# Attention in a transformer block on one core: scores in three float32r passes over split queries and keys, reciprocals of the sums turned by a store and a load

## The chip, the core and the metric

The kernel runs on one core of a Trainium2 chip. A core has a matrix engine (TensorE, "PE" in the profile, with its weight loads as "PEld"), a vector engine (VectorE, "DVE"), a scalar engine (ScalarE, "ACT"), a general engine (GpSimd, "POOL") and a queue engine that issues transfers (SyncE, "SP"). Each works through its own instructions in program order, and they wait for one another by semaphores. Transfers run on 16 DMA engines. The metric is the device time of one execution in microseconds: 1033.1 before, the median of 3 runs (1032.53 to 1033.29).

## What is computed

One layer of a diffusion transformer, in float32: a modulated RMSNorm, an input projection, a token mixer (half pooling, half neighbourhood attention), an output projection, and a squared-ReLU MLP. The change lies in the attention of 1024 tokens on a 16 x 64 grid, with 8 heads of 64 and 256 context keys that every query sees:

```python
def row_block(r):
    ...
    s_loc = jnp.einsum('bnqhd,brnkhd->bhnqrk', q_r, k_b).astype(jnp.float32) * scale
    ...
    s_loc = jnp.where(col_mask, s_loc + bias.astype(jnp.float32), -jnp.inf)
    s_ctx = jnp.einsum('bnqhd,bkhd->bhnqk', q_r, k_ctx).astype(jnp.float32) * scale
    s = jnp.concatenate([s_loc.reshape(B, H, NA_NCB, NA_QB, n_loc), s_ctx], axis=-1)
    p = jax.nn.softmax(s, axis=-1).astype(v.dtype)
    p_loc = p[..., :n_loc].reshape(B, H, NA_NCB, NA_QB, kh, NA_KB)
    p_ctx = p[..., n_loc:]
    o = (jnp.einsum('bhnqrk,brnkhd->bnqhd', p_loc, v_b)
         + jnp.einsum('bhnqk,bkhd->bnqhd', p_ctx, v_ctx))
    return o.reshape(B, GRID_W, H, Dh)
```

## The kernel before

The large products run in float32r, a form of the operands in which a float32 value is split into a high part (a cast, `high_part` or `high`, on ScalarE) and a low part (value minus high, on VectorE). `three` (L197 to L200) multiplies high by high, high by low and low by high into one bank. The attention's own matmuls stay in float32.

*Ahead of the attention.* The projection of queries and keys is a seven-product scheme over quarter matrices; `kept_product` (L911 to L923) adds and subtracts the products into the pages `kT` (keys by head pair) and `q` (queries in blocks of 512 columns). The last products of the queries, P7 and P4, are computed by `last_query`: P7 just ahead of the loop, P4 within its first two turns. `tables(j)` (L867 to L883) makes the bias tables of head pair j: it loads U from `in_rpb` on SP's queue, and Pool subtracts it from a mask, 12 operations of 128 columns.

*The loop.* Pages of 128 x 1024 come from one pool of 33 (`page`), handed on when the last reader of the old content is done. A unit i is a head pair j = i / 8 and a column tile m = i % 8, 32 units in all; a tile's keys are those of itself and its neighbours (384 local columns for an inner tile, 256 at the edges) and 256 context columns. The loop runs N + 4 = 36 turns. Turn i holds, in this order:

- `tables` of the next pair, where m is 2; loads of output weights at turns 8, 16, 26 and 28 (`LOADS`); the six loads of the second half of the output weights at turn 32
- `weighed(i-4)` (L1070, VectorE): values times the reciprocals, into the heads' page
- modulation work: `mod_gate` at turn 4 (which stores `ga`), `column_sums` at turns 5 and 8 (storing and gathering `gsc`/`sc` and `gsh`/`s`), four accumulating transfers `y<-y` on Pool's queue in turns 1 and 2, the loads `ss<-y` on SP's at turns 5 and 6
- `low`, `mixed_split` (turns 8, 16, 24, 32) and `weight_split`: casts on ScalarE (L1082) and subtractions on VectorE (L1083)
- `scores(i)`: matmuls (L984, two heads on two halves of the rows), then on VectorE per head one custom operation, bias added and the extreme value found (L998)
- `turn(i-2)` (L1026): transposes of the exponentials, 64 x 64, and of the shares; `fifth_kept(i-2)` (L1040, ScalarE) copies what lies beside the banks
- `exps(i)` (L1007, ScalarE), with `turn_kept(i-2)` (L1045) in between: one copy of transposes on ScalarE, one on VectorE
- `share(i-1)`: the reciprocals of the sums (L1011) and their spread over 64 columns per head (L1013), both on VectorE
- `values(i-3)` (L1060, TensorE)

The program fixes the order within TensorE, ScalarE, VectorE and SP (`in_order`) and, over the loop, within Pool (`first_pool`). After the loop the mixed tokens go through the output projection (`out_sums`, `out_load`, accumulating `add_to` transfers on Pool's queue), whose first casts of the second half are `to_0h`, `to_1h`.

Of the kernel before, what the change touches and what calls it, by code (L numbers as in the profile page):

```python
# [80 lines left out]
def hybrid_block(ctx, tc, x, ctx_in, w_mod, b_mod, gp1, gp2, w_in, pool_w, rpb, w_out, w1, w2, vectors,  # L81
# [189 lines left out]
    with tc.tile_pool(name="ps1", bufs=6, space=PSUM) as ps1, tc.tile_pool(name="tmp1", bufs=3) as tmp:  # L271
# [614 lines left out]


        kT, qT = [None] * 4, [[None] * 2 for _ in range(4)]
        by_tile = lambda t: t.rearrange("p (m t) -> p m t", t=P)
        query = lambda j, b: by_tile(qT[j][b])[:, :, ::-1]  # L890

# [39 lines left out]
        with in_order(ET.PE, ET.Pool, ET.Activation, ET.DVE, ET.SP) as pooling:  # L931
            banks = {of: [bank(f"p{of}{j}") for j in range(2)] for of in "KQ"}
            use(-1)
            for step, (n, of, j) in enumerate([(n, of, j) for n, of in products for j in range(2)]):
                half_product(n, of, j, banks[of])
                use(step)
                if step in (5, 9, 17):
                    name = {5: "S1", 9: "S4", 17: "S3"}[step]
                    parts = token_operand(name, sraw[name])
                if step in (5, 7, 9, 11, 17, 19):  # L940
                    next(parts)
                    next(parts)
# [12 lines left out]

    with (
# [9 lines left out]
        sides = (pa[:, 256:448], pz[:, :192])  # L966


        def scores(i):
            j, m = units[i]  # L970
            inner = 0 < m < NM - 1
            n = NKEY if inner else 4 * P
            o = 1 if m == 0 else 0
            q = qT[j][m // 4]
            cols = slice((m % 4) * P, (m % 4 + 1) * P)
            heads = [slice(e * HD, (e + 1) * HD) for e in range(2)]
            S = [ps_s.tile([P, 1024], F32, tag="S", name=f"S{j}_{m}_{e}") for e in range(2)]
            if inner:
                parts = ((128, kT[j][:, (m - 1) * P : (m + 2) * P]), (512, kc[:, j, :]))
            else:  # L980
                parts = ((0, kc[:, j, :]), (256, kT[j][:, (m + o - 1) * P : (m + o + 1) * P]))
            for c0, keys in parts:
                for e, hs in enumerate(heads):
                    nc.tensor.matmul(S[e][:, c0 : c0 + keys.shape[1]], q[hs, cols], keys[hs], start=True, stop=True)  # L984
            halves = lambda a: a.rearrange("p (a b) -> p a b", a=2)
            for e in range(2):
                t = tabs[j % 2][e]
                sp = att.tile([P, NKEY], F32, tag="sp", name=f"sp{j}_{m}_{e}", bufs=6)[:, :n]
                if inner:
                    s, bt, to = S[e][:, 128:768], t[:, :NKEY], sp  # L990
                else:
                    s, to = halves(S[e][:, 0:512]), halves(sp)
                    if o:
                        bt = halves(t[:, 2 * P : 8 * P])[:, :, P:]
                    else:
                        bt = halves(t[:, NLOC : NLOC + 512])
                nm = sm(f"nm_{i}_{e}", 1, 6)
                nc.vector.tensor_tensor_reduce(out=to, in0=s, in1=bt, scale=1.0, scalar=BIG, op0=add, op1=ALU.min,  # L998
                                               accum_out=nm)
                probs[i, e] = sp  # L1000
                least[i, e] = nm
# [7 lines left out]
        def share(i):  # L1009
            ri = sm(f"ri_{i}", 2, 2)  # L1010
            nc.vector.reciprocal(ri, sums[i])  # L1011
            shares[i] = att.tile([P, P], F32, tag="ri", name=f"rb{i}", bufs=2)
            nc.vector.tensor_copy(shares[i].rearrange("p (e t) -> p e t", e=2),  # L1013
                                  ri.rearrange("p (e o) -> p e o", o=1).to_broadcast([P, 2, HD]))

        def turn(i):
            inner = 0 < units[i][1] < NM - 1
            t = [bank(f"T{i}_{h}") for h in range(2)]  # L1020
            turned[i] = t
            halves = [slice(h * HD, (h + 1) * HD) for h in range(2)]

            def both(to, src):
                for h, hs in enumerate(halves):
                    nc.tensor.transpose(to(h), src(hs), ident[hs, hs])  # L1026

            both(lambda h: sides[h][:, :HD], lambda hs: shares[i][hs])
            for e in range(2 if inner else 0):
                both(lambda h: sides[h][:, (e + 1) * HD : (e + 2) * HD], lambda hs: probs[i, e][hs, 4 * P : 5 * P])  # L1030
            for c in range(4):
                for e in range(2):
                    o = (4 * e + c) * HD
                    both(lambda h: t[h][:, o : o + HD], lambda hs: probs[i, e][hs, c * P : (c + 1) * P])

        def fifth_kept(i):
            n = (3 if 0 < units[i][1] < NM - 1 else 1) * HD
            fifths[i] = att.tile([P, 384], F32, tag="px", name=f"px{i}", bufs=4).rearrange("p (h t) -> p h t", h=2)
            for h in range(2):
                nc.scalar.copy(fifths[i][:, h, :n], sides[h][:, :n])  # L1040

        def turn_kept(i, h, copy):
            if h == 0:
# [4 lines left out]
        def values(i):  # L1048
            j, m = units[i]
            vc = [vcp[:, 0:512], vcp[:, 512:1024]]  # L1050
            if 0 < m < NM - 1:
                vs = vb[m - 1 : m + 2] + vc
            else:
                o = 1 if m == 0 else 0
                vs = vc + vb[m + o - 1 : m + o + 1]
            cols = slice((i % 2) * P, (i % 2 + 1) * P)
            for c, v in enumerate(vs):
                for e in range(2):
                    f = (2 * j + e) * HD
                    nc.tensor.matmul(pa[e * HD : (e + 1) * HD, cols], v[:, f : f + HD],  # L1060
                                     turns[i][:, e, c] if c < 4 else fifths[i][:, :, (e + 1) * HD : (e + 2) * HD],
                                     start=(c == 0), stop=(c == len(vs) - 1))


        def weighed(i):
            j, m = units[i]
            if m == 0:
                heads[j] = page(f"f{j}")
            to = heads[j].rearrange("p (m h t) -> p m h t", h=2, t=HD)[:, m, ::-1, ::-1]
            nc.vector.tensor_tensor(to, pa[:, (i % 2) * P : (i % 2 + 1) * P].rearrange("p (h t) -> p h t", h=2),  # L1070
                                    fifths[i][:, :, :HD], mul)

        N = len(units)

# [77 lines left out]
        with in_order(ET.PE, ET.Activation, ET.DVE, ET.SP) as projected:  # L1152

            def last_query(n, j):
                half_product(n, "Q", j, last_queries)
                kept_product(n, "Q", j, last_queries[j])

            for j in range(2):
                last_query("P7", j)
            for i in range(N + 4):  # L1160
                if i < N and units[i][1] == 2 and units[i][0] < 3:
                    tables(units[i][0] + 1)
                if i in LOADS:
# [827 lines left out]
```

## Time and profile before

| | |
|---|---|
| median of 3 runs | 1033.1 us (1032.53 to 1033.29) |
| the profiled execution: span | 1030.8 us |
| TensorE busy | 1017.8 us, 99% of the span |
| VectorE busy | 751.8 us, 73% |
| ScalarE busy | 543.7 us, 53% |
| Pool busy | 110.7 us, 11% |
| attention loop, first scores of unit 0 to those of unit 31 | 218.90 to 319.35 us |

A span is what lies between the first and the last instruction of the profiled execution; the runs' times are taken around it. Rows of a timeline read: start in us, length in us, engine, line of the kernel, operation, output <- inputs, partitions x elements, number of instructions in the group, and in brackets the idle time before it with what ended it. Matmuls overlap with the next one, so the distance between two starts, not the length, is what one costs. In the chain of waits each piece has its start, its length and the work. Rows of transfers give queue, number, size of each and median time from issue to landing.

### The profile page before, as it was taken

How to read it: one execution, taken by the hardware profiler on the slowest of the kernel's cores; microseconds unless marked ns; L12 is line 12 of the kernel's file. 1: busy time of each engine (PE TensorE's matmuls, PEld its weight loads, DVE VectorE, ACT ScalarE, POOL GpSimd, SP SyncE). 2: the span in 40 equal slices, each digit the busy share in tenths (PEclk: the TensorE clock that was granted, in tenths of full speed). 3: DMA queues.
4: the chain of work that ended last, by engine and by line, in shares of the span. 5: the costliest groups of instructions: out<-in, count | busy, mean ns of one | idle time of the engine just before them, and what ended most of it. 6: DMA issues, size and time to landing. Idle time of an engine off the chain costs nothing.

```text
span 1030.8 us, 15588 instructions
## 1 busy us (share of the span) xinstructions
PE 1017.8 (99%) x5782; PEld 834.2 (81%) x5782; DVE 751.8 (73%) x1187; ACT 543.7 (53%) x941; POOL 110.7 (11%) x168
## 2 busy tenths in 40 slices
PE   8999999999999999999999999999999999999997
PEld 6788888877887888888888888888888888888885
DVE  5588767858996587878998887855766666547576
ACT  7573255328887556776655544555543334334431
POOL 3011200244311311310000000000000000000001
PEclk9999999999999999999999999999999999999999
DMA  9999798632337866795786666637967766555556
GB/s 343 332 255 338 246 265 296 204 86 80 72 95 194 203 180 200 253 237 168 267 269 210 204 210 214 205 122 241 327 220 271 248 226 220 202 180 189 176 182 211
DMA packets 123132, 222.68 MB, mean 216 GB/s; under 512 B 9456, under 2 KB 55152, under 8 KB 123056
## 3 DMA queue, kind: packets, MB, share of 16 engines
q1 hardware_dynamic: 96560, 171.14, 50.4%
q0 software_dynamic: 9360, 19.58, 9.5%
q10 hardware_dynamic: 17136, 30.97, 8.0%
q8 instruction: 45, 0.74, 0.3%
q14 instruction: 31, 0.25, 0.1%
HBM read 168.16 MB, written 52.45 MB: 214 GB/s over the span
## 4 chain that ended last, share of the span: by engine, by line
PE 95%; DMA 2%; ACT 1%; DVE 1%; issue 0%; SPq 0%; DVEq 0%; POOLq 0%; ACTq 0%
PE pu L449 4%; PE S L984 4%; PE pa L1060 3%; PE phv L198 3%; PE phz L198 3%; PE phx L198 3%; PE pyx L198 3%; PE phx L200 3%; PE phv L199 3%; PE phx L199 3%; PE pyx L199 3%; PE pyx L200 3%; PE pyv L199 3%; PE pyv L198 3%; PE pyz L199 3%; PE pyz L198 3%
## 5 line engine op out<-in xcount | busy, mean ns | idle before, releaser
L1007 ACT ACTIVATE sp<-sp,nm 128x640 f32<-128x640 f32 (+1 forms) x64 | 51.4, 803 | 20.0 <-DVE nm L998 19.6
L1577 ACT ACTIVATE c<-c 128x512 f32<-128x512 f32 x48 | 30.3, 632 | 47.0 <-DVE c L1697 28.2
L146 ACT CAST wpS<-S 128x512 fp32r<-128x512 f32 x64 | 38.7, 616 | 26.4 <-PE phv L200 9.2
L198 PE MATMUL phx<-thB,wpA 128*128 128x512 f32 x128 | 50.2, 392 | 0.0
L200 PE MATMUL phx<-thB,wpA 128*128 128x512 f32 x128 | 49.8, 389 | 0.0
L199 PE MATMUL phx<-tlB,wpA 128*128 128x512 f32 x128 | 49.8, 389 | 0.0
L152 DVE TENSOR_TENSOR wpS<-S,wpS 128x512 fp32r<-128x512 f32 x64 | 43.4, 685 | 8.3 <-ACT wpS L146 8.3
L998 DVE CUSTOM_DVE_ANT_0 sp<-S,tab 128x640 f32<-128x640 f32 (+1 forms) x56 | 42.9, 803 | 8.8 <-PE S L984 7.3
L1578 ACT ACTIVATE c<-c 128x512 f32<-128x512 f32 x48 | 30.3, 631 | 15.1 <-DVE sa L1660 12.3
L140 POOL TENSOR_TENSOR ry<-vy,nhalf 128x1 f32<-128x1 f32 x8 | 5.9, 740 | 280.7 <-DVE vy L138 280.7
L198 PEld LDWEIGHTS phx<-thB,wpA 128*128 128x128 f32 x128 | 24.0, 188 | 5.5 <-ACT s L1628 0.5
L984 PE MATMUL S<-kT,q 64*128 64x384 f32 (+1 forms) x128 | 27.9, 495 | 0.3 <-DVE nm L998 0.3
L200 PEld LDWEIGHTS phx<-thB,wpA 128*128 128x128 f32 x128 | 24.0, 188 | 5.0
L199 PEld LDWEIGHTS phx<-tlB,wpA 128*128 128x128 f32 x128 | 24.0, 188 | 4.9
L1060 PE MATMUL pa<-pt,v 128*64 128x128 f32 x352 | 25.9, 279 | 0.6 <-ACT px L1040 0.2
L1045 DVE COPY pt<-T 128x512 f32<-128x512 f32 x32 | 22.0, 686 | 5.5 <-PE T L1026 5.5
L198 PE MATMUL phv<-thT,wpA 128*128 128x512 f32 x64 | 25.1, 392 | 0.0
L198 PE MATMUL phz<-thB,wpS 128*128 128x512 f32 x64 | 25.0, 391 | 0.0
L200 PE MATMUL phv<-thT,wpA 128*128 128x512 f32 x64 | 24.9, 389 | 0.0
L199 PE MATMUL phv<-tlT,wpA 128*128 128x512 f32 x64 | 24.9, 389 | 0.0
L200 PE MATMUL phz<-thB,wpS 128*128 128x512 f32 x64 | 24.9, 389 | 0.0
L199 PE MATMUL phz<-tlB,wpS 128*128 128x512 f32 x64 | 24.9, 389 | 0.0
(1100 smaller groups left out, 3359.7 us busy)
## 6 DMA issues: line engine op xcount, KB each, us to landing
b<-in_w SPq DMA_DIRECT2D x64, 512.0 KB, 4.2
hrS<-hdS SPq DMA_DIRECT2D x32, 512.0 KB, 5.1
hrA<-hdA SPq DMA_DIRECT2D x24, 512.0 KB, 5.5
wm<-in_w_mod SPq DMA_DIRECT2D x16, 512.0 KB, 9.7
wa_0w<-in_w SPq DMA_DIRECT2D x16, 512.0 KB, 5.3
wa_1w<-in_w SPq DMA_DIRECT2D x16, 512.0 KB, 4.5
hdA<-c ACTq DMA_DIRECT2D x32, 256.0 KB, 2.8
hdS<-sa ACTq DMA_DIRECT2D x32, 256.0 KB, 2.7
```

Of the source, the lines that this page charges most:

```text
L146: nc.scalar.copy(hi, src)
L152: nc.vector.tensor_tensor(lo, src, hi.bitcast(F32), sub)
L198: nc.tensor.matmul(ps, ahi, bhi, start=first, stop=False, skip_group_check=more)
L199: nc.tensor.matmul(ps, ahi, blo, start=False, stop=False, skip_group_check=more)
L200: nc.tensor.matmul(ps, alo, bhi, start=False, stop=last, skip_group_check=more)
L449: nc.tensor.matmul(pus[b][j], wk(wgt, k, low, j * P, P), r, start=(k == 0 and n == 0), stop=(k == KT - 1 and n == 2))
L984: nc.tensor.matmul(S[e][:, c0 : c0 + keys.shape[1]], q[hs, cols], keys[hs], start=True, stop=True)
L998: nc.vector.tensor_tensor_reduce(out=to, in0=s, in1=bt, scale=1.0, scalar=BIG, op0=add, op1=ALU.min, accum_out=nm)
L1007: nc.scalar.activation(sp, sp, AF.Exp, bias=least[i, e], scale=-1.0, accum_out=sums[i][:, e : e + 1])
L1060: nc.tensor.matmul(pa[e * HD : (e + 1) * HD, cols], v[:, f : f + HD], turns[i][:, e, c] if c < 4 else fifths[i][:, :, (e + 1) * HD : (e + ...
L1577: nc.scalar.activation(r, src, AF.Relu)
L1578: nc.scalar.activation(r, r, AF.Square)
```

## The change

Queries and keys are split into high and low parts: `parts_of` casts 512 columns on ScalarE and subtracts on VectorE, or on Pool where the engine is given. There are 16 such splits, and the context keys' page is split once, 128 x 1024. One split of keys and one of queries are made in the projection stage, four right ahead of the loop, two in turn 2 on VectorE, and eight in turns 3 to 6, whose subtractions go to Pool. `scores` runs three passes over each part. Since a key page now has 512 columns, tiles 3 and 4, whose keys lie in two pages, have three parts in place of two.

The reciprocals are no longer spread by a VectorE copy and transposed by TensorE: `share` stores the 128 x 2 reciprocals to memory on SP's queue, transposed, and `spread`, one turn later, loads each head's row into 64 partitions, two transfers on SP's queue. `weighed` multiplies by what was loaded. `turn` loses its transposes of the shares, and `fifth_kept` copies 128 columns in place of 192 for inner units and nothing for edge units.

```diff
+        keys, queries, kcs = {}, {}, []
+
+        def parts_of(to, j, b, small=False, engine=None):
+            name = f"{'k' if to is keys else 'q'}P{j}_{b}"
+            src = kT[j][:, b * 512 : (b + 1) * 512] if to is keys else qT[j][b]
+            t = whl.tile([P, 1024], F32R, tag="hl", name=name) if small else page(name, F32R)
+            hi, lo = to[j, b] = t[:, :512], t[:, 512:]
+            nc.scalar.copy(hi, src)
+            (engine or nc.vector).tensor_tensor(lo, src, hi.bitcast(F32), sub)
...
+                if step == 10:
+                    kcs += [page(f"kc{n}", F32R) for n in "hl"]
+                    split(kcp, *kcs)
+                if step == 20:
+                    parts_of(keys, 0, 0)
+                if step == 22:
+                    parts_of(queries, 0, 0, True)
...
-            if inner:
-                parts = ((128, kT[j][:, (m - 1) * P : (m + 2) * P]), (512, kc[:, j, :]))
-            else:
-                parts = ((0, kc[:, j, :]), (256, kT[j][:, (m + o - 1) * P : (m + o + 1) * P]))
-            for c0, keys in parts:
-                for e, hs in enumerate(heads):
-                    nc.tensor.matmul(S[e][:, c0 : c0 + keys.shape[1]], q[hs, cols], keys[hs], start=True, stop=True)
+            t0, t1 = (m - 1, m + 2) if inner else (m + o - 1, m + o + 1)
+            at = 128 if inner else 256
+            local = []
+            for b in range(2):
+                b0, b1 = max(t0, 4 * b), min(t1, 4 * b + 4)
+                if b0 < b1:
+                    local.append((at + (b0 - t0) * P, [a[:, (b0 - 4 * b) * P : (b1 - 4 * b) * P] for a in keys[j, b]]))
+            parts = local + [(512, ck)] if inner else [(0, ck)] + local
+            for c0, k in parts:
+                for n_q, n_k in ((0, 0), (0, 1), (1, 0)):
+                    for e, hs in enumerate(heads):
+                        nc.tensor.matmul(S[e][:, c0 : c0 + k[0].shape[1]], q[n_q][hs, cols], k[n_k][hs],
+                                         start=(n_q + n_k == 0), stop=(n_q == 1))
...
-            shares[i] = att.tile([P, P], F32, tag="ri", name=f"rb{i}", bufs=2)
-            nc.vector.tensor_copy(shares[i].rearrange("p (e t) -> p e t", e=2),
-                                  ri.rearrange("p (e o) -> p e o", o=1).to_broadcast([P, 2, HD]))
+            inverse[i] = dram.tile([2, P], F32, tag=f"inv{i % 6}", name=f"inv{i}")
+            nc.sync.dma_start(inverse[i].rearrange("e t -> t e"), ri)
+
+        def spread(i):
+            shares[i] = att.tile([P, P], F32, tag="ri", name=f"rb{i}", bufs=4)
+            for e in range(2):
+                nc.sync.dma_start(shares[i][e * HD : (e + 1) * HD], inverse[i][e : e + 1, :].to_broadcast([HD, P]))
...
-            both(lambda h: sides[h][:, :HD], lambda hs: shares[i][hs])
...
-            n = (3 if 0 < units[i][1] < NM - 1 else 1) * HD
-            fifths[i] = att.tile([P, 384], F32, tag="px", name=f"px{i}", bufs=4).rearrange("p (h t) -> p h t", h=2)
+            if not 0 < units[i][1] < NM - 1:
+                return
+            fifths[i] = att.tile([P, 256], F32, tag="px", name=f"px{i}", bufs=4).rearrange("p (h t) -> p h t", h=2)
             for h in range(2):
-                nc.scalar.copy(fifths[i][:, h, :n], sides[h][:, :n])
+                nc.scalar.copy(fifths[i][:, h], sides[h])
...
             nc.vector.tensor_tensor(to, pa[:, (i % 2) * P : (i % 2 + 1) * P].rearrange("p (h t) -> p h t", h=2),
-                                    fifths[i][:, :, :HD], mul)
+                                    shares[i].rearrange("p (h t) -> p h t", h=2), mul)
...
+            parts_of(keys, 0, 1, True)
+            parts_of(queries, 1, 0, True)
+            parts_of(keys, 1, 0, True)
+            parts_of(keys, 1, 1)
+            later = [(to, 2, b, True) for b in range(2) for to in (keys, queries)]
+            later += [(to, 3, b, False) for b in range(2) for to in (keys, queries)]
             for i in range(N + 4):
+                if i == 2:
+                    for j in range(2):
+                        parts_of(queries, j, 1)
+                if 3 <= i < 7:
+                    for _ in range(2):
+                        parts_of(*later.pop(0), nc.gpsimd)
...
+                if 1 < i <= N + 1:
+                    spread(i - 2)
                 if 0 < i <= N:
                     share(i - 1)
```

More of the change, by code (lines that the diff above doesn't have):

```diff
@@ L965, in hybrid_block @@
         pa, pz = (ps_o.tile([P, 512], F32, tag=n, name=n) for n in ("pa", "pz"))
-        sides = (pa[:, 256:448], pz[:, :192])
+        sides = (pa[:, 256:384], pz[:, :128])
+        inverse = {}
         def scores(i):
@@ L973, in scores @@
             o = 1 if m == 0 else 0
-            q = qT[j][m // 4]
+            q = queries[j, m // 4]
+            ck = [a[:, j * CTX : (j + 1) * CTX] for a in kcs]
             cols = slice((m % 4) * P, (m % 4 + 1) * P)
@@ L1026, in both @@
                     nc.tensor.transpose(to(h), src(hs), ident[hs, hs])
-            both(lambda h: sides[h][:, :HD], lambda hs: shares[i][hs])
             for e in range(2 if inner else 0):
-                both(lambda h: sides[h][:, (e + 1) * HD : (e + 2) * HD], lambda hs: probs[i, e][hs, 4 * P : 5 * P])
+                both(lambda h: sides[h][:, e * HD : (e + 1) * HD], lambda hs: probs[i, e][hs, 4 * P : 5 * P])
             for c in range(4):
@@ L1060, in values @@
                     nc.tensor.matmul(pa[e * HD : (e + 1) * HD, cols], v[:, f : f + HD],
-                                     turns[i][:, e, c] if c < 4 else fifths[i][:, :, (e + 1) * HD : (e + 2) * HD],
+                                     turns[i][:, e, c] if c < 4 else fifths[i][:, :, e * HD : (e + 1) * HD],
                                      start=(c == 0), stop=(c == len(vs) - 1))
```

## The prediction

> **What bounds the kernel now.** I read the page's head and its chain of waits first, then the chain through the attention stage, a table of busy time by stage, and last one unit of the loop instruction by instruction. A unit is one column tile of one pair of heads; there are 32, and the loop starts one per turn.
>
> ```profile
> span 1030.8 us, 15588 instructions
> ...
> PE 95%; DMA 2%; ACT 1%; DVE 1%; issue 0%; SPq 0%; DVEq 0%; POOLq 0%; ACTq 0%
> ```
>
> 95% of the chain is TensorE work, so time taken off TensorE comes off the end, as long as the others can follow. In the chain through the stage (start, length, what), these are the scores of units 8 and 31:
>
> ```profile
> 247.44 1.06 PE S L984 x8
> ...
> 319.35 1.06 PE S L984 x8
> ```
>
> 23 units in 71.91 us: 3.127 us each. The stage's table (PE, PEld, DVE, ACT, Pool busy) tells what stands behind TensorE:
>
> ```profile
> 240.00:260.00 20.00, 20.00 (x306) 16.03 (x304) 17.34 (x54) 17.42 (x48) 10.30 (x22) 1.00 0.14 28
> ```
>
> VectorE and ScalarE are each busy 87% of it: there is little room before they would bind. One unit on TensorE and then on VectorE:
>
> ```profile
> 262.84 0.92 PE L984 MATMUL S<-kT,q 64*128 64x384 f32 x4
> ...
> 263.59 0.60 PE L984 MATMUL S<-kcT,q 64*128 64x256 f32 x4
> ...
> 264.02 0.22 PE L1026 MATMUL pa<-ident,rb 64*128 64x64 f32 x1
> ...
> 266.04 0.92 PE L984 MATMUL S<-kT,q 64*128 64x384 f32 x4
> ```
> ```profile
> 264.22 0.82 DVE L998 CUSTOM_DVE_ANT_0 sp<-S,tab 128x640 f32<-128x640 f32 x1
> ...
> 266.32 0.16 DVE L1011 RECIPROCAL ri<-su 128x2 f32<-128x2 f32 x1
> ...
> 266.65 0.28 DVE L1070 TENSOR_TENSOR f<-pa,px 128x128 f32<-128x128 f32 x1
> ```
>
> From start to start: 0.75 us for the local scores, 0.43 for those on the context, 2.02 for transposes and values; 3.20 in all. VectorE's part of a unit runs from 264.22 to 266.93 (266.65 + 0.28), 2.71 us.
>
> **The change, part by part.** *Scores.* Each f32 matmul stands in the trace as two instructions (x4 for two heads), whose heads run side by side; the change makes three float32r passes of it. The nearest float32r rows:
>
> ```profile
> 85.16 0.28 PE L690 MATMUL pkc<-hc,wk0l 128*128 128x256 f32 x1
> 85.28 0.39 PE L690 MATMUL pkc<-hc,wk0h 128*128 128x512 f32 x1
> 85.50 0.28 PE L690 MATMUL pkc<-hc,wk0l 128*128 128x256 f32 x1
> ```
>
> Above, two f32 passes of 256 columns take 0.43, or 0.84 ns a column and pass; 384 would take 0.64, and the other 0.11 of the 0.75 is the first pass's start. In float32r 256 columns take 0.12 and 512 take 0.22, 0.43 to 0.47 ns a column. An inner unit becomes 3 x (0.165 to 0.18) + 3 x (0.11 to 0.12) + 0.11 = 0.93 to 1.01, against 1.18: -0.2. By the same rates the 8 edge units (256 + 256 columns) win 0.14; 8 others cross the new 512-column pages and have three short parts, which is worth between nothing and 0.17, taken as 0.09. The mean over 16, 8 and 8 units is -0.16. The transposed pair of shares goes too, one of 33 steps between 264.02 and the values: -0.06 as the trace spaces these first pairs. TensorE's own period becomes 2.91; 2.8 to 3.05 are its ends, since no row has float32r on 64 rows with two heads side by side.
>
> *The other engines.* VectorE loses the copy of the shares (0.14 to 0.23), ScalarE two narrow slices, so VectorE comes to about 2.5 a unit and ScalarE, whose 87% of 3.127 is 2.72, to a little less than that. They can follow 2.91, but not much below 2.75.
>
> *The splits, and what waits for Pool.* The 16 splits of 512 columns cost a cast and a subtraction each. These rows have the same shapes, and show where the loop stood (ScalarE, then VectorE):
>
> ```profile
> 247.89 0.62 ACT L1082 CAST mix<-f 128x512 fp32r<-128x512 f32 x1
> ```
> ```profile
> 227.77 0.15 DVE L1011 RECIPROCAL ri<-su 128x2 f32<-128x2 f32 x1
> ...
> 249.87 0.69 DVE L1045 COPY pt<-T 128x512 f32<-128x512 f32 x1
> ...
> 251.00 0.68 DVE L1083 TENSOR_TENSOR mix<-f,mix 128x512 fp32r<-128x512 f32 x1
> ```
>
> Those in the projection stage run under TensorE's products: nothing (without that cover 3 x 0.65). Four subtractions ahead of the loop, 4 x 0.68 = 2.7, stand on VectorE before the first unit's bias; TensorE still has a projection product of 3 us between units 0 and 1, so some 0.6 to 0.9 reaches the first reciprocal (227.77 becomes 228.4), and the two of the third turn add 1.4. The eight of turns 3 to 6 go to Pool, two a turn, with two casts (1.24) a turn on ScalarE. What Pool and SP's queue do there now:
>
> ```profile
> 221.28 4.95 POOL L883 TENSOR_TENSOR tab<-msk,U 128x128 f32<-128x128 f32 x12 [10.47 <-DMA U<-in_rpb]
> 226.17 1.69 POOL L188 DMA_DIRECT2D y<-y  x2
> 234.52 1.99 POOL L253 DMA_DIRECT2D ga<-acca  x4 [6.67 <-DVE acca L247]
> 238.68 1.91 POOL L253 DMA_DIRECT2D gsc<-accsc  x4 [2.17 <-ACT accsc L621]
> 242.22 0.93 POOL L623 DMA_DIRECT2D sc<-gsc  x1 [1.63 <-DMA gsc<-accsc]
> ```
> ```profile
> 216.89 1.19 SPq L876 DMA_DIRECT2D U<-in_rpb  x2
> ```
>
> SP runs in program order, and the store of unit 0's reciprocals comes ahead of the load of U for the second pair's bias table. So that load, issued at 216.89 now, waits for the first reciprocal and the store's issue: about 228.4 + 0.15 + 0.42 = 229.0. Pool's table started 4.39 after the issue (221.28), so it starts at 233.4, ends at 238.4, and the two y accumulations end at 240.1; only then come the subtractions. One of 512 columns on Pool has no row: the table's 128-column ones come every 4.95/12 = 0.41, so four times that, 1.65, is the upper bound; the lower is VectorE's 0.68 for that shape, since nothing here shows Pool ahead of VectorE. I take 1.35, near the upper end, whose rows are Pool's own, less 0.3 for what is paid once instead of four times. In Pool's order four subtractions precede the ga stores, two the gsc stores, and two follow the sc gather: the sixth ends at 240.1 + 6 x 1.35 + 2.0 = 250.2, the seventh at 240.1 + 7 x 1.35 + 1.99 + 1.91 + 1.63 + 0.93 = 256.0, the eighth at 257.4.
>
> Who waits: a page is handed on when its last reader is done, and by the program's order the mix cast of the eighth turn (247.89) needs the seventh subtraction's page, and the copy of unit 6's transposes (249.87) the eighth's. They would come 8.1 and 7.5 late. Behind them on ScalarE and VectorE stand the next unit's exponentials and biases, and TensorE waits for those. A second path is nearly as late: the ss load of turn 6 waits on SP for the ga stores (issued by 240.1 + 4 x 1.35 + 2.0 = 247.5), and the shares of unit 4 stand behind it. I take 7.5 us of delay at unit 8, with 3 (subtractions of 0.68: the seventh at 251.3) and 10 (1.65: 8 x 0.3 more) as ends.
>
> The Trainium skill, "GPSIMD Engine Reference", section 3.1 (Elementwise — side-by-side cycle accounting), has a two-input operation on Pool at about 2.6 cycles an element, 4497 ns for 2048 elements. By that I estimate 1.2 us for 512; the eighth would end at 256.2 and the sum would be 1.2 lower. By the same estimate 128 elements need about 0.28, and the trace's 0.41 is above it, so I stay with the row.
>
> *The reciprocals' way over memory.* Each unit's 128 x 2 values are stored as 256 separate elements; two loads spread them over 64 partitions each a turn later. On SP the loads of unit k wait for its store to have landed, and the next store is queued behind them. So a turn of SP is store to landing + two issues. Nearest rows: a small store and a gather (size, time to landing), and the issues of a small broadcast load (least, median and most ns):
>
> ```profile
> gsc<-accsc POOLq DMA_DIRECT2D x4, 1.0 KB, 1.6
> ...
> sc<-gsc POOLq DMA_DIRECT2D x1, 4.0 KB, 3.0
> ```
> ```profile
> L243 SPq DMA_DIRECT2D gpa<-in_gp x4: 347/416/698, 201.9 to 203.5; - x4
> ```
>
> 1.6 in whole rows, 3.0 for 1024 single elements: for 256 elements I take 2.0, plus 2 x 0.42, plus some 0.1: 2.9 a unit (2.4 to 3.9). There is time in a unit's own account: a reciprocal is due 3.5 after its scores (266.32 - 262.84), the weighting 0.56 after those of three turns later, so 3 x 2.9 - 3.1 = 5.6 for store, issues and loads, 2.0 + 0.8 + 2.0 with loads like stores.
>
> *The end of the loop.* Six loads of 512 KB for the output weights stand between the last reciprocals' transfers on SP. Before, the first was issued and, after an accumulation by Pool, used by ScalarE at
>
> ```profile
> 308.06 0.37 SPq L1143 DMA_DIRECT2D to_0w<-in_w_out  x1
> ```
> ```profile
> 340.57 1.05 ACT L146 CAST to_0h<-to_0w 128x1024 fp32r<-128x1024 f32 x1
> ```
>
> Behind unit 30's store (its reciprocal is due 3.5 after 319.35, so 323 and the delay) the cover of 32.5 us shrinks to some 17, which still has to hold a load and an accumulation. I put 1.0 on it (0 if both fit, 4 if they need 21).
>
> *The sum.* From unit 8 on the period is the greater of TensorE's 2.91 and SP's 2.9, which take turns: I take 2.95, 0.177 less than now, times 24 = 4.2 back. 1030.8 + 7.5 - 4.2 + 1.0 = 1035.1 of span. The runs' median, 1033.1, is 2.3 above the profiled span; with that, 1037.4.
>
> **The rivals.** *SP sets the period.* If a store takes 2.6 or more to land, SP's turn is 2.6 + 0.84 + 0.1 = 3.5, over what TensorE needs today. Then nothing comes back and 24 x 0.35 = 8 is added: 1033.1 + 7.5 + 8 = 1048.6. For it: the 3.0 of single elements, and the loads of 512 KB among which these small ones run. Against it: there are a quarter as many elements. It decides from a landing of 2.2 (period 3.13). The Trainium skill, "DMA: Bandwidth & Descriptors", speaks for this rival: under Specifications it has transfers below 512 bytes as read-modify-write, and under Rules for kernel authors many small transfers are to be made one large one. No row here shows a 4-byte store.
>
> *Faster: the delay is hidden and TensorE keeps its gain.* If Pool's subtraction is below 0.9, the eighth ends by 253.8, 3.9 late, as long as the path by the ss load is no later; and with passes of 0.16 and 0.11 and a landing below 1.8 (whole rows have 1.6), the period falls to 2.8, TensorE's lower end. Then 24 x 0.327 = 7.8 comes back: 1033.1 + 4.5 - 7.8 = 1029.8. For it: TensorE is the chain at 95%. Against it: 0.41 for 128 columns would have to be mostly fixed cost.
>
> *The scores don't get shorter.* Three passes are fewer than two f32 ones only if float32r on half the rows, with short columns, keeps 0.47 ns a column. If it went at the rate of f32, the 1.07 of the passes would grow by half, 0.54, less 0.06 for the shares: period 3.6, 1033.1 + 7.5 + 24 x 0.48 = 1052. Against it: the rows at 256 columns keep the rate.
>
> **How the numbers follow.** The forecast's own range: delay 5.5 to 9.9, period 2.9 to 3.1: 1033 to 1044. Chances: forecast 0.48, SP's period 0.25, faster 0.20, scores no shorter 0.04; 0.03 for what I don't see. The range, 1029.5 to 1050, takes in the lower end of all costs (1033.1 + 3 - 6.6 at a period of 2.85) and SP's rival. A difference counts from 0.2%, about what a measurement of this kernel can tell: 1031.0 and 1035.2. Below that: 0.15 from the faster case and 0.02 of the forecast; between: 0.05 of the faster case and 0.13 of the forecast; the rest is slower, 0.65.
>
> **What would show it.** The second pair's U load issued near 229 and its table starting near 233; the mix cast of the eighth turn idle behind Pool and near 255; unit 8's scores at 255, not 247.4. Pool's subtraction of 512 columns at 1.35. From unit 8 on 2.95 from scores to scores, scores at 0.95 to 1.0. SP's stores landing in 2.0; over 2.2, and weighting idle behind rb, would show the first rival. I am wrong in the main step if unit 8 is less than 3 late, or if the period stays at 3.1 for a reason other than SP.

## The result, and the profile after

The changed kernel takes 1246.24 us (median of 4 runs, 1245.58 to 1249.75) against 1033.12: a ratio of 1.2071, interval 1.2056 to 1.2086. It is 213 us slower, where 4 were forecast. The page of the profile after, its span, its chain by engine and by line:

```profile
span 1247.9 us, 15982 instructions
...
PE 72%; DMA 23%; SPq 3%; DVE 1%; issue 1%; ACT 0%; DVEq 0%; POOLq 0%; ACTq 0%
DMA inv<-ri 20%; PE pu L449 4%; DMA rb<-inv 3%; SPq L1042 2%; PE phv L198 2%; PE phz L198 2%; PE phx L198 2%; PE pyx L198 2%; PE pyv L200 2%; PE phv L199 2%; PE phz L199 2%; PE phx L199 2%; PE pyz L200 2%; PE pyx L200 2%; PE phx L200 2%; PE
```

A fifth of the chain is one kind of transfer, the store of the reciprocals (`inv<-ri`). All of the loss lies in the attention loop: the last unit's weighting, on VectorE, first before and then after:

```profile
337.35 0.28 DVE L1070 TENSOR_TENSOR f<-pa,px 128x128 f32<-128x128 f32 x1
```
```profile
555.12 0.29 DVE L1098 TENSOR_TENSOR f<-pa,rb 128x128 f32<-128x128 f32 x1 [2.89 <-DMA rb<-inv]
```

It comes 217.8 us later, and the spans differ by 217.1. What SP waited for in the loop (line, releaser, us in total, times, longest), and two turns of SP's queue:

```profile
SPq L1042 <- DMA inv<-ri: 227.5, 30, 9.5
```
```profile
406.63 1.09 SPq L1042 DMA_DIRECT2D rb<-inv  x2
407.77 0.59 SPq L1037 DMA_DIRECT2D inv<-ri  x1
416.20 1.09 SPq L1042 DMA_DIRECT2D rb<-inv  x2
417.39 0.53 SPq L1037 DMA_DIRECT2D inv<-ri  x1
```

A store is issued at 407.77, the loads behind it at 416.20, 8.43 later, when it has landed; two issues of 1.09 together, and the next store goes at 417.39. A turn is 9.6 us, and one unit is done per turn. TensorE is busy for half of such a stretch (PE, PEld, DVE, ACT, Pool busy, the granted clock, share of the DMA engines):

```profile
400.00:440.00 40.00, 20.21 (x208) 17.51 (x208) 11.25 (x30) 11.19 (x30) 5.87 (x12) 0.63 0.26 28
```

Its granted clock is 0.63 here, 1.00 in the same loop before; but TensorE is not what SP's turn waits for. Transfers of the stage, first before and then after (number, size, median from issue to landing):

```profile
wor<-in_w_out SPq DMA_DIRECT2D x4, 512.0 KB, 3.7
...
U<-in_rpb SPq DMA_DIRECT2D x6, 244.5 KB, 3.9
...
ga<-acca POOLq DMA_DIRECT2D x4, 1.0 KB, 2.4
```
```profile
rb<-inv SPq DMA_DIRECT2D x64, 32.0 KB, 3.5
wor<-in_w_out SPq DMA_DIRECT2D x4, 512.0 KB, 10.7
...
U<-in_rpb SPq DMA_DIRECT2D x6, 244.5 KB, 11.3
...
inv<-ri SPq DMA_DIRECT2D x32, 1.0 KB, 8.4
...
ga<-acca POOLq DMA_DIRECT2D x4, 1.0 KB, 10.2
```

The 1 KB store lands in 8.4 us, and `wor`, `U` and `ga`, which have nothing to do with it, land 7 to 8 us later than before, the last of them on Pool's queue. Not every transfer does: `gsh` lands in 1.8 (the median), against 2.2 before.

### The profile page after: what moved, and what is told of

The parts are those of the page before. It is cut to its first block, busy times and chain, and to the rows that moved or that the text cites. A ratio compares the mean times of both kernels' runs of the same rounds, so it can differ in the third digit from the quotient of the medians.

```text
span 1247.9 us, 15982 instructions
## 1 busy us (share of the span) xinstructions
PE 1073.1 (86%) x5894; PEld 887.8 (71%) x5894; DVE 754.0 (60%) x1164; ACT 548.1 (44%) x942; POOL 120.1 (10%) x176
## 4 chain that ended last, share of the span: by engine, by line
PE 72%; DMA 23%; SPq 3%; DVE 1%; issue 1%; ACT 0%; DVEq 0%; POOLq 0%; ACTq 0%
DMA inv<-ri 20%; PE pu L449 4%; DMA rb<-inv 3%; SPq L1042 2%; PE phv L198 2%; PE phz L198 2%; PE phx L198 2%; PE pyx L198 2%; PE pyv L200 2%; PE phv L199 2%; PE phz L199 2%; PE phx L199 2%; PE pyz L200 2%; PE pyx L200 2%; PE phx L200 2%; PE pyv L198 2%
## 5 line engine op out<-in xcount | busy, mean ns | idle before, releaser
L1054 PE MATMUL pa<-ident,sp 64*128 64x64 f32 x48 | 11.4, 334 | 116.3 <-DVE f L1098 116.3
L1098 DVE TENSOR_TENSOR f<-pa,rb 128x128 f32<-128x128 f32 x32 | 9.3, 292 | 147.1 <-DMA rb<-inv 145.5
L1054 PEld LDWEIGHTS pa<-ident,sp 64*128 64x128 f32 x48 | 6.9, 196 | 122.1 <-DVE f L1098 122.1
L1088 PE MATMUL pa<-pt,v 128*64 128x128 f32 x352 | 42.5, 404 | 15.2 <-DVE f L1098 15.2
L1088 PE MATMUL pa<-pt,vc 128*64 128x128 f32 x160 | 23.1, 407 | 29.6 <-DVE f L1098 29.6
L1088 PEld LDWEIGHTS pa<-pt,v 128*64 128x64 f32 x352 | 32.1, 209 | 18.0 <-DVE f L1098 15.7
L1088 PEld LDWEIGHTS pa<-pt,vc 128*64 128x64 f32 x160 | 15.6, 213 | 30.9 <-issue 17.2
L1007 PE MATMUL S<-kP,qP 64*128 64x256 f32 (+2 forms) x240 | 35.1, 415 | 2.2 <-DVE nm L1022 2.0
L1007 PEld LDWEIGHTS S<-kP,qP 64*128 64x128 f32 x240 | 25.5, 266 | 10.7 <-issue 6.5
L1054 PE MATMUL T<-ident,sp 64*128 64x64 f32 x512 | 30.9, 286 | 0.0
```

The costliest lines, as they stand in the source:

```text
L1007: nc.tensor.matmul(S[e][:, c0 : c0 + k[0].shape[1]], q[n_q][hs, cols], k[n_k][hs], start=(n_q + n_k == 0), stop=(n_q == 1))
```

## The experiments

The theory from this profile: SP's turn, store to landing plus two issues, sets the period, and the store is slow because of how its 256 elements fall in memory. Rivals: that the scores or the splits cost a part; that the landing is long because of the queue; that any store of so many small pieces is that slow.

**Which half of the change.** The changed kernel with the reciprocals' old way (e1), and the kernel before with the new one (e2):

```diff
-            inverse[i] = dram.tile([2, P], F32, tag=f"inv{i % 6}", name=f"inv{i}")
-            nc.sync.dma_start(inverse[i].rearrange("e t -> t e"), ri)
+            shares[i] = att.tile([P, P], F32, tag="ri", name=f"rb{i}", bufs=2)
+            nc.vector.tensor_copy(shares[i].rearrange("p (e t) -> p e t", e=2),
+                                  ri.rearrange("p (e o) -> p e o", o=1).to_broadcast([P, 2, HD]))
...
```

> The changed kernel with the reciprocals' old way: VectorE's copy and TensorE's transposes, nothing stored. Theory 'the store' (all of the loss is the way over memory): 1029 to 1040 us, a delay of 3 to 7 at unit 8, then about 2.95 from scores to scores. Rival 'the scores' (short float32r passes, splits or Pool's subtractions cost a good part of the 213 us): above 1060.

> The kernel before with only the reciprocals' new way (store, two loads, no transposes of shares), scores in float32 and no splits. Theory 'the store': 1235 to 1255 us, 9.4 us from scores to scores, SP's chain of store and loads in the chain of waits as in the changed kernel. Rival 'the scores': below 1200.

e1: 1034.95 us beside 1032.59 for the kernel before, ratio 1.0024 (1.0015 to 1.0034). e2: 1260.62, 6 above the end of what was expected, and ratio 1.2207 (1.2181 to 1.2233). The way over memory alone makes the loss; splits and float32r passes together cost 2.4 us. (e2 is 14 us slower than the whole change; why isn't shown.) Scores in e1's chain, then one of the kernel before:

```profile
313.01 1.25 PE S L1007 x18
...
316.20 1.08 PE S L1007 x12
...
322.22 0.91 PE S L1007 x12
```
```profile
316.15 1.28 PE S L984 x8
```

x18 are tiles with three parts, x12 with two; the last is an edge tile, 1.06 before (unit 31 in the prediction's rows). In these rows the passes win 0.20, 0.03 and 0.15. What they lose again stands, in part, in the windows of the first turns, e1 and then before:

```profile
218.00:240.00 22.00, 18.76 (x214) 14.31 (x213) 18.10 (x42) 13.44 (x34) 12.72 (x21) 1.00 0.36 95
240.00:260.00 20.00, 17.90 (x312) 15.51 (x310) 17.05 (x46) 17.04 (x47) 14.46 (x24) 1.00 0.32 81
```
```profile
218.00:240.00 22.00, 21.70 (x224) 15.36 (x225) 14.76 (x40) 12.31 (x33) 9.88 (x21) 1.00 0.52 144
```

TensorE is idle for 5.3 us of 42, against 0.3.

**The queue.** The stores issued from ScalarE's queue, with 6 buffers for the reciprocals (e3):

```diff
-            nc.sync.dma_start(inverse[i].rearrange("e t -> t e"), ri)
+            nc.scalar.dma_start(inverse[i].rearrange("e t -> t e"), ri)
```

> The changed kernel with the stores issued from ScalarE's queue, the loads left on SP's, and 6 buffers for the reciprocals in place of 2, so that stores overlap. Theory 'SP's turn' (the store lands in 8.4 us and SP waits for it each turn; taken apart, what is left is one unit's own way round: 8.4 + 1.1 + 3.5 for store, issues and loads against three periods less 3.1): a period near 5.4, about 1105 us (1085 to 1130). Theory 'queue' (another queue makes the store land in 2 to 3 us): 1033 to 1045. Theory 'the stores follow each other in the DMA engines': a period of 8 or more, above 1190.

1171.81 us, which none of the three had. Its transfers:

```profile
rb<-inv SPq DMA_DIRECT2D x64, 32.0 KB, 7.6
...
inv<-ri ACTq DMA_DIRECT2D x32, 1.0 KB, 9.1
```

On a queue of its own the store lands no sooner. Nor does it when no other store is ahead of it; the first one in e3's chain (start, length):

```profile
227.98 7.95 DMA inv<-ri
```

So the queue isn't the cause. SP no longer holds the next store back, and the reciprocals have more buffers; together this gives 74 of the 213 us. The loads, 3.5 in the change, now take 7.6: the stores hold them up elsewhere than in SP's order.

**How the elements fall in memory.** Six stores in the changed kernel, otherwise alike: 128 pieces of 8 bytes side by side (e4); 256 elements, each in 512 bytes of its own (e5) or in 64 (e8); two whole rows (e6); one column, 128 elements in one row (e7); and one column with each 16 neighbours in a row of their own (e9). In all of them the output is weighted by the wrong numbers.

```diff
 e4
+nc.sync.dma_start(inverse[i].rearrange("e t -> (e t)").rearrange("(p x) -> p x", x=2), ri)
 e5; e8 with 16 in place of the last P
+spaced = [dram.tile([2, P, P], F32, tag=f"inv{n}", name=f"inv{n}") for n in range(6)]
+nc.sync.dma_start(spaced[i % 6][:, :, 0].rearrange("e t -> t e"), ri)
 e6
+nc.vector.tensor_copy(row[:, 0:1], ri[:2, 0:1])
+nc.sync.dma_start(inverse[i], row)
 e7
+nc.sync.dma_start(inverse[i].rearrange("e t -> t e"), ri[:, :1])
 e9, spaced of [8, P]
+nc.sync.dma_start(spaced[i % 6][:, :16], ri[:, :1])
```

> The changed kernel with the reciprocals stored untransposed, 128 pieces of 8 bytes side by side (the loads read the same 1 KB as before, so the output's weights are in the wrong places). SP's turn is landing + 1.1. Theory 'pieces': half the pieces, landing 4 to 5, period 5 to 6, 1095 to 1130 us. Theory 'same line': still some 128 small writes into two rows of 512 bytes, landing 4 to 8. Theory 'bytes or fixed' (the landing doesn't hang on the pieces): 8.4 and 1246.

> The changed kernel with each of the 256 elements stored into 512 bytes of its own; the loads read rows of which one element is a reciprocal and the others are ones (the output is weighted wrongly). Theory 'same line' (small writes into one 512 bytes wait for each other): landing 2 to 3, period 3.1 to 4.1, 1035 to 1065 us. Theory 'pieces' (256 small writes cost the same wherever they go): landing about 8.4, 1246 us within 15.

> The changed kernel with a store of two whole rows of 512 bytes in place of the 256 elements, still behind the reciprocal (one element of it goes into the row; the rest of the row is ones, so the output is weighted wrongly). This is the forecast's store. Theory 'pieces' and theory 'same line' alike: landing 1.6 to 2.2, period 2.95 to 3.2, 1034 to 1042 us. If the loads or the wait for landing as such are the cause, it stays above 1060.

> The changed kernel with only the first head's reciprocals stored, 128 elements of 4 bytes into one row of 512 bytes, which both loads read (the second head is weighted by the first head's sums). Theory 'pieces': as the 128 pieces of 8 bytes, landing 4 to 5, 1095 to 1130 us. Theory 'same line': 128 writes into one row take as long as 128 each into two rows, landing 7 to 8.4, above 1200.

> As the run with 512 bytes for each stored element, but with 64 bytes for each: eight elements now share 512 bytes (in the change 128 share them). Elements in rows of 512 bytes of their own landed in 3.6 us (median), 128 in one row in 9.0. Theory 'what shares 512 bytes waits' (unit of 512): between the two but near the fast end, landing 3 to 4.5, 1065 to 1090 us, slower than with 512 each. Theory 'unit of 64 bytes or less': as with 512 each, 1060 to 1075. If only the spread over more memory matters and not the sharing, landing 5 or more, above 1100.

> As the run with one column (128 elements of 4 bytes, which landed in 9.0 us within one row of 512 bytes), but each 16 neighbouring elements, 64 bytes, go into a row of 512 bytes of their own, eight rows. The loads read the first row; the output is weighted wrongly. Theory 'unit of 64 bytes' (small writes wait for those into the same 64 bytes; 16 share them here as in the change): landing stays at 8 to 9, 1240 to 1270 us. Theory 'unit of 512 bytes' (16 share a row in place of 128): landing 3 to 4.5, 1060 to 1095 us.

The store's row among the stage's transfers, of e7, e4, e8 and e5 in turn:

```profile
inv<-ri SPq DMA_DIRECT2D x26, 0.5 KB, 9.0
```
```profile
inv<-ri SPq DMA_DIRECT2D x32, 1.0 KB, 4.8
```
```profile
inv<-ri SPq DMA_DIRECT2D x32, 1.0 KB, 3.2
```
```profile
inv<-ri SPq DMA_DIRECT2D x32, 1.0 KB, 3.6
```

For e9 and e6 the landings stand as pieces of the chain of waits (start, length), first the longest and the shortest of 15 in e9's, then one of e6's and, from its end, a load:

```profile
319.91 5.56 DMA inv<-ri
...
336.66 1.84 DMA inv<-ri
```
```profile
303.35 1.56 DMA inv<-row
...
334.92 13.03 DMA rb<-inv
```

| kernel | pieces of a store | in one row of 512 bytes | landing, us | time, us |
|---|---|---|---|---|
| the change | 256 x 4 bytes | 128 | 8.4 | 1246.2 |
| e7 | 128 x 4 | 128 | 9.0 | 1268.6 |
| e4 | 128 x 8 | 64 | 4.8 | 1136.6 |
| e9 | 128 x 4 | 16 | 1.8 to 5.6 in its chain | 1096.4 |
| e8 | 256 x 4 | 8 | 3.2 | 1075.0 |
| e5 | 256 x 4 | 1 | 3.6 | 1071.5 |
| e6 | 2 x 512 | whole | 1.5 to 2.4 in its chain | 1046.9 |

It isn't the number of pieces: e7 has half the change's and lands as late, e5 as many and lands in 3.6. With 128 and 64 writes in one row of 512 bytes the landing goes by that number; from 16 down to 1 no order is left (pieces of the chain last from 2.1 to 5.0 in e5 and from 2.0 to 5.5 in e8, much as in e9), and e8 and e5 lie too close to tell their theories apart. That e9 is some 20 us slower than both isn't explained. e9 keeps the 64 bytes together that the change has, and still drops most of the way: if it is the sharing of some stretch of memory that counts, the stretch is larger than 64 bytes. 512 fits these rows, but 128 and 256 would order them in much the same way, and no run separates the three. Each piece also comes from a partition of its own, so the number of writes into a row can't be told here from the number of partitions that write it. The spread over more memory alone is not the cause: the change, e4 and e6 all fill 1 KB, and land in 8.4, 4.8 and about 1.6. e5 was 6 us above its expected end, and e6 5 above: a fast store does not bring the forecast back (below).

**Do the stores cost without a wait?** A first kernel (m1) had seven kinds of store, in turn, in the kernel before, with no reader; two more (m2, m3) had one kind each:

```diff
 m2
+            nc.sync.dma_start(dram.tile([2, P], F32, tag=f"st{i}", name=f"st{i}").rearrange("e t -> t e"), ri)
 m3
+            nc.sync.dma_start(dram.tile([2, P, P], F32, tag=f"st{i}", name=f"st{i}")[:, :, 0].rearrange("e t -> t e"), ri)
```

> The kernel before, in which every unit also stores something that nobody reads, in seven kinds taken in turn: A the 128 x 2 reciprocals transposed, 256 single elements into two rows of 512 bytes (as the change does); B the same untransposed, 128 pieces of 8 bytes side by side; C as A, but with each element in its own 512 bytes; D one column only, 128 single elements; E two rows of 512 bytes; F as A, on ScalarE's queue; G a load of one 512-byte row into 64 partitions. Reciprocals have 8 buffers, so nothing waits for a store soon. Theory 'pieces' (a store costs by its number of small pieces): A, C and F land in about 8.4 us, B and D in 4 to 6, E in 2. Theory 'same line' (small writes into the same 512 bytes wait for each other): C lands in 2 to 3 while A and F keep 8.4, B is near A. Theory 'queue' (the landing is long because SP's queue is shared with large loads and because the next transfers hang on it): A lands in 2 to 3.5 here, and F differs from A. G should land in 2 to 3.5.

> The kernel before, whose every unit also stores its reciprocals as the change does (256 elements into two rows of 512 bytes); nobody reads them, and 8 buffers keep the reciprocals from waiting soon. Theory 'the stores hold the DMA engines, whoever waits for them': other transfers of the stage (U, ss, ga, wor) land 5 to 10 us late, 1070 to 1130 us. Rival 'only SP's wait for the landing costs': 1033 to 1040.

> The same with each element stored into 512 bytes of its own. Theory 'writes into the same 512 bytes hold the engines': other transfers land as before, 1033 to 1042 us. Rival 'any 256 small writes hold them': as the run with two rows.

m1 could not tell its seven kinds apart, since the trace has no landing for them; it took 1073.48 us. In its chain the load of U, issued right behind the first store of kind A (12.7 us; its table on Pool started 4.4 after the issue before):

```profile
228.42 12.71 DMA U<-in_rpb
```

m2 took 1093.38 (ratio 1.0591, 1.0561 to 1.0622), m3 1032.38 (0.9996, 0.9985 to 1.0007). A piece of m2's chain (`gsh` landed in 2.2 in the kernel before), then m3's transfers:

```profile
267.05 15.35 DMA gsh<-accsh
```
```profile
U<-in_rpb SPq DMA_DIRECT2D x6, 244.5 KB, 4.1
...
st<-ri SPq DMA_DIRECT2D x32, 1.0 KB, 1.9
```

One stretch of the loop in m2, then in m3 (the last two numbers are the busy share of the 16 DMA engines and the GB/s that they move):

```profile
300.00:320.00 20.00, 14.45 (x178) 11.58 (x178) 10.43 (x29) 9.39 (x26) 2.48 (x5) 0.83 0.87 46
```
```profile
300.00:320.00 20.00, 20.00 (x302) 16.21 (x298) 17.59 (x53) 16.98 (x46) 2.58 (x3) 1.00 0.54 114
```

So 32 stores of 1 KB that nobody reads cost 61 us when their elements share rows, and nothing that can be measured when they don't. Other transfers are held up: m2's engines are busy for 0.87 of the time and move 46 GB/s, m3's for 0.54 and move 114. In m3 the stores land in 1.9 us (median).

It is not the stores' own pieces that keep the engines busy. The packets (the pieces that the engines move) in the 1.3 us from the first store's issue, in e3, where the elements share rows, and in m3 (queue, packets, MB, busy share; then the landing in m3):

```profile
q10 hardware_dynamic: 272, 0.00, 11.3%
```
```profile
q1 hardware_dynamic: 272, 0.00, 11.3%
...
st<-ri SPq DMA_DIRECT2D x1, 1.0 KB, 1.6
```

The same 272 packets take the same share of the engines' time, and from there to 233.4 the store's queue in e3 moves nothing. But e3's store lands 7.95 us after its issue and m3's 1.6. The difference lies behind the last packet; what happens there the traces don't show.

**The end of the loop.** e6 with the six loads of output weights moved behind the last shares' loads on SP's queue (e10):

```diff
-                if i == N:
+                if i == N + 1:
                     t1 = [out_load(f"to1_{kk}w", kk, 1) for kk in (0, 1)]
...
```

> The run with whole rows stored (1046.85 us), with the six loads of the output weights moved behind the last shares' loads on SP's queue. Theory 'at the end the shares' loads stand behind 3 MB' (13 us from issue to landing for unit 30's, TensorE idle 5.4 of 20 us behind it): 1038 to 1042.5 us, no wait of more than 4 us for a share at the end. Rival 'the weights come late instead': 1045 to 1050.

1046.99 against 1046.85, one run each: the rival. In e6 the 13.03 us above are unit 30's shares behind 3 MB, with TensorE idle for 5.4 us; moved, the shares are in time, and the weights are not. e6's window, then e10's next one and its chain:

```profile
340.00:360.00 20.00, 14.56 (x67) 11.66 (x66) 7.33 (x11) 5.14 (x9) 2.64 (x3) 0.83 0.78 180
```
```profile
360.00:380.00 20.00, 15.62 (x57) 12.06 (x56) 13.29 (x22) 13.76 (x26) 5.28 (x6) 0.83 1.06 224
```
```profile
345.88 12.91 DMA to_3w<-in_w_out
```

**Better places for the splits?** Both with the reciprocals' old way: one split a turn, the last eight wholly on Pool (v1); two made during the projection, the others one a turn (v3).

```diff
 v1
+            plan = {1: packed(keys, 0, 1), 2: (queries, 0, 1), 3: packed(queries, 1, 0), 4: packed(keys, 1, 0),
+                    5: (keys, 1, 1), 6: (queries, 1, 1)}
+            (turns 8 to 11, 13, 15, 17, 19: pairs 2 and 3, cast and subtraction on Pool)
 v3
+                if step == 21:
+                    parts_of(keys, 1, 0)
+                if step == 23:
+                    parts_of(queries, 1, 0)
```

> The changed scores with the reciprocals' old way, and the splits placed otherwise: none right ahead of the loop; one each in turns 1 to 6 on ScalarE and VectorE; the eight of pairs 2 and 3 wholly on Pool (cast and subtraction), one each in turns 8 to 11 and 13, 15, 17, 19. With the change's placing this way's loop took 3.0 us a unit at its end, TensorE idle for 6.9 us between 218 and 340 (0.9 before), and 1034.95 us. Theory 'the splits' place costs what the passes win': idle 1 to 3 us, 1028.5 to 1031.5. Rival 'the passes win too little, 3.0 is what VectorE and ScalarE can hold': 1032 to 1035.

> The changed scores with the reciprocals' old way, and two of the four splits ahead of the loop made two or three products earlier, under TensorE's projection work; one more moved to turn 1, the two of turn 2 to turns 2 and 3, and the eight whose subtractions are Pool's to one a turn in turns 4 to 11. Theory 'the first turns' splits cost what the passes win' (TensorE idle for 5.3 us between 218 and 260 in the run with the change's placing): idle there 2 to 3.5, 1030 to 1033 us. Rival 'ScalarE and VectorE have no room for the splits wherever they lie': 1034 to 1037.5.

v1: 1037.49 us (ratio 1.0043, 1.0030 to 1.0057); v3: 1040.69 (1.0077, 1.0063 to 1.0091). Each misses both of its ranges on the slow side, so the theory falls twice, and the rivals' figures with it. v3 is slower than e1 against its own kernel before; v1's interval touches e1's. v1 between 260 and 280, then v3's chain there:

```profile
260.00:280.00 20.00, 18.57 (x327) 16.35 (x325) 19.34 (x53) 17.42 (x45) 18.52 (x28) 1.00 0.33 68
```
```profile
263.29 3.92 DMA U<-in_rpb
...
267.28 4.96 POOL tab L883 x12
```

v1's splits fill Pool and VectorE (18.5 and 19.3 of 20 us) in the turns where they come; in v3 the third pair's U is loaded only at 263.29 and its table begins at 267.28, 13 us later than in the kernel before (254.08). That these make the loss fits the rows, but no run isolates it. No kernel here beats the one before. Untried is to gather the reciprocals into whole rows on the chip and store those; e6, which stores whole rows without the work of gathering, was at 1046.9.

## Why the prediction was wrong

The step that failed is "The reciprocals' way over memory": "1.6 in whole rows, 3.0 for 1024 single elements: for 256 elements I take 2.0". The store landed in 8.4. The ends were no bounds: one row was a write of a few larger pieces (not of whole rows: the trace has each of those 1 KB stores as 16 packets of 64 bytes), the other a gather, which reads; neither writes many pieces into one row of memory. The mechanism was named as the first rival, SP's store and loads setting the period, with the point from which it decides (2.2); its price, 2.6 + 0.84 + 0.1, was mis-sized in the same term, and 24 x 0.35 became 31 turns of about 10, some 6.9 longer than a unit took before. The two issues were 1.1 in place of 0.84.

The second thing that was missing has no term in the sum: a store that holds up others. U's landing of 11.3 and ga's of 10.2 are not SP's order; m2 prices it at 61 us with no reader. The 2.0 itself came true only in m3, 1.9, where elements have room and nothing waits for them. In the changed kernel the same spaced store (e5), which there is issued right behind two loads on SP's queue, took 3.6, above the 2.2 from which the rival decides.

The other terms can be read from e1, which leaves the way over memory out, and from e6, which has it with the fast store. The scores were sized about right: -0.20, -0.03 and -0.15 us measured, -0.2, -0.09 and -0.14 forecast. Pool's subtraction of 512 columns, 1.35 forecast:

```profile
233.97 1.27 POOL L897 TENSOR_TENSOR kP<-kT,kP 128x512 fp32r<-128x512 f32 x1 [2.42 <-ACT kP L896]
```

The estimate of 1.2 by the Trainium skill, "GPSIMD Engine Reference", section 3.1 is as near as mine.

The delay came as forecast in e6. Its table and the last of the eight subtractions on Pool, then the first scores of unit 8 before, and of units 8 and 31 in e6, all by the timeline:

```profile
232.81 4.96 POOL L883 TENSOR_TENSOR tab<-msk,U 128x128 f32<-128x128 f32 x12 [11.82 <-DMA U<-in_rpb]
...
255.13 1.29 POOL L897 TENSOR_TENSOR qP<-q,qP 128x512 fp32r<-128x512 f32 x1
```
```profile
247.37 0.70 PE L984 MATMUL S<-kcT,q 64*128 64x256 f32 x4
```
```profile
254.26 0.39 PE L1010 MATMUL S<-kch,qP 64*128 64x256 f32 x2
...
326.99 0.38 PE L1010 MATMUL S<-kch,qP 64*128 64x256 f32 x2
```

The table starts at 232.8 (forecast 233.4), the eighth subtraction ends at 256.4 (257.4), and unit 8 is 6.9 late (7.5).

The gain did not come, and this is a second step that failed: "They can follow 2.91", of VectorE and ScalarE. From unit 8 to unit 31 e6 takes 72.73 us, 3.16 a unit, in place of 2.95. In e1, with nothing on SP's way, unit 8 is 3.7 late and a unit takes 3.09 (251.07 to 322.15 by the same view): the prediction's own sign of being wrong, a period of 3.1 for a reason other than SP. Some shares of e1's chain from 246 to 325, and VectorE and ScalarE (third and fourth of the busy times) in one stretch of it:

```profile
by line: PE pa L1084 22.7%; PE S L1007 18.4%; ACT sp L1031 11.7%; DVE sp L1022 9.9%; PE T L1050 7.7%; issue 7.3%; ACT pt L1069 4.8%; PE pa L1050 3.4%; DVE pt L1069 2.3%; DVE f L1094 2.2%; ACT px L1064 2.0%; ACT mix L1106 1.3%; ACT wo_0h L11
```
```profile
280.00:300.00 20.00, 19.22 (x353) 17.33 (x350) 18.66 (x53) 17.46 (x48) 6.46 (x12) 1.00 0.26 46
```

TensorE has little more than half of that chain, and VectorE is busy for 93% of the stretch, some 2.9 us a unit where 2.5 was put down (e1 keeps the copy of the shares, for which the forecast took off 0.14 to 0.23). Which of its operations would have to go for 2.91 isn't shown.

So it is luck that e1 comes near the sum. Delay and gain together were forecast as 7.5 - 4.2 = +3.3 us at unit 31's scores, and e1's come at 322.22, +2.9 on 319.35; but that is 3.7 of delay, without U behind the first store, less 0.8 of gain. The whole time of e1, +2.4, is no better a sign.

"The end of the loop" was sized at 1.0, with 4 as its end, and it named the casts of the weights. In e6, where the store is fast, TensorE is idle for 1.5 + 5.4 us from 320 to 360 (0.2 before), and first the shares wait, not the weights. e10 shows that either order costs as much. e6 is 7.7 late at unit 31's scores (3.3 forecast) and 14.3 at the end of its span: the gain that did not come is 4.4 and the end of the loop 5.6 over its term, which makes up the 9.5 us by which e6 stands above the forecast, within 0.6.

The Trainium skill, "DMA: Bandwidth & Descriptors", was cited for the rival: under Specifications, transfers below 512 bytes are read-modify-write. No run here shows a read-modify-write, or that 512 bytes is the size that counts. What they show is that small writes are dear where many share a row of 512 bytes (8.4 to 9.0 us with 128, 4.8 with 64), and cost nothing that can be measured where each has a row and nothing waits for them (1.9, and 1032.38 us).

## What to carry to other kernels

Before a column is turned into a row by a store, count the writes that fall into one 512-byte row of memory: 128 took 8 to 9 us here, and transfers beside them came 7 to 8 us late. Where a bound for a cost comes from neighbouring rows, see that they do the same thing in the same direction: here a gather's time said nothing about a scatter's. And a wait that a queue makes in program order (store, landing, loads, next store) is a loop of its own; its turn belongs beside the busiest engine's before anything else is summed. Last, a sum that comes out right can hide a delay and a gain that are both wrong: each term belongs beside its own row, as at unit 8 here.

## What was not expected of the hardware

Transfers that nobody waits for cost 61 us by where their bytes go, and an identical number of bytes in as many pieces, spread out, cost nothing (1093.38 and 1032.38 us). The hold reaches other queues: ga on Pool's took 10.2 us in place of 2.4. The dear store's own packets are done as fast as the cheap one's, within 1.3 us; the 7.95 us against 1.6 lie behind them. And with TensorE idle half of the time its granted clock was 0.63 in a stage that had run at 1.00.
